# Transposed activations high, all weight buffers low in one pool, and products of zeros until the first weights

## The chip, the cores and the metric

The kernel runs on one core of a Trainium2 chip. The metric is device time in microseconds of one execution; a row of three such times is the measurement of the kernel before. Five engines work side by side, each on its own queue in the order in which the program lists its instructions: TensorE (PE: matrix products and transposes), VectorE (DVE), ScalarE (ACT), GpSimd (POOL) and SyncE (SP), which issues most DMA transfers. An instruction that has to wait holds up all behind it on its engine.

## What is computed

Two layers of a decoder on 256 tokens of width 1024, all in float32. Layer 0 mixes by sparse attention and differential attention, layer 1 by block-sparse attention; each is followed by an MLP of width 4096 with a squared ReLU.

```python
def rms_norm(x, g):
    xf = x.astype(jnp.float32)
    y = xf * lax.rsqrt(jnp.mean(xf * xf, axis=-1, keepdims=True) + EPS)
    return (y * g.astype(jnp.float32)).astype(x.dtype)

def sqrelu_mlp(hn, w1, w2):
    return jnp.square(jax.nn.relu(hn @ w1)) @ w2
...
    for i in range(DEPTH):
        hn = rms_norm(x, norm_mix[i])
        ...
            mix = odd_mixer(hn, od_w_in[o], od_w_out[o], bias_table)
        x = x + mix
        x = x + sqrelu_mlp(rms_norm(x, norm_mlp[i]), mlp_w1[i], mlp_w2[i])
    return rms_norm(x, norm_final)
```

## The kernel before

**Products.** Every float32 operand is split into a high part and a low rest in a reduced format (`hi`, `lo`), and a product is the sum of three: high by high, high by low, low by high (`mm3`, L552 to L554). An instruction row such as `ps<-whi,xTh` names the bank of the result and the two operands. The tokens lie in two tiles of 128 (t=0 and t=1).

**Weights.** The weights lie in one long array, in pieces of 128 rows by up to 1024 columns, in the order in which they are used. `loads` fetches a piece into one of five raw buffers; `splits` copies its high part on ScalarE (L492) and subtracts it on VectorE (L495). The parts go into six pairs of buffers. Three pairs (`whi`, `wlo`, the list `near`) lie low in the pool `hot`, at the start of each partition; three (`vhi`, `vlo`, the list `far`) lie high in the pool `consts`. In between lie the transposed x (`xTh`, `xTl`) and the attention's or MLP's transposed results (`mTh`, `mTl`). Each piece is marked as stationary or moving in its products, or as free; `region` lets a stationary piece take only a `far` pair, a moving one only a near pair (or a half of `mT` when that is lent out by `spare_m`), and a free one any. Pieces 4 and 5 of an output projection go into the two halves of `xT` (`ROOM`, `spare_x`).

**From x to its transpose.** `to_xT` scales x by the norm's weight on VectorE into a buffer P (L599), `turn_x` transposes four 128 by 128 blocks on TensorE (L615), copies the high part on ScalarE (L537) and the low part on VectorE (L543). The factor of the root mean square is made on its own (`rvar`, L585 to L587) and used later. The first norm is another: `first_norms` spreads the norm's weight over 128 partitions by two products with a row of ones (L919), takes the root mean square by a power on POOL (L579), and scales by both at once (L935).

**Order.** A planner (`Plan`) runs at build time. It holds an estimated duration for every step and starts on each engine the step of the lowest urgency number that is ready by its own clock; the instructions are written in that order. So a change of a buffer's rule changes the order of everything that the planner then sees ready earlier or later. `add_to_x` (L1335) adds an output projection's bank to x. `mlp` begins with two up-projections in which the tokens are stationary (`unit_N`), one for each token tile, and their results are transposed on TensorE (L1426).

**The start.** A tile of zeros is set, and six products of zeros of 512 columns (`WARM`) run on TensorE before the norm weight arrives.

Of the kernel before, what the change touches and what calls it, by code (L numbers as in the profile page):

```python
# [24 lines left out]
OP = mybir.AluOpType  # L25
# [48 lines left out]
def _blocks(ins):  # L74
# [44 lines left out]
    free = set(range(len(out)))  # L119

    def mlp(l):
# [7 lines left out]
        free.update(range(len(out), len(out) + TAIL))  # L129
# [3 lines left out]
    free.update(range(len(out), len(out) + 4))  # L133
# [5 lines left out]
    free |= set(range(len(out), len(out) + 4))  # L139
    out += [r(f["od_w_out"][0], i) for i in range(4)]  # L140
    mlp(1)
    cut, still = [], []
    for i, b in enumerate(out):
        stationary = None if i in free else b.ndim == 4
        b = np.ascontiguousarray(b).reshape(128, -1)
        k = 1 if b.shape[1] <= 1024 else 2
        cut += [np.ascontiguousarray(c) for c in np.split(b, k, 1)]
        still += [stationary] * k
    return cut, still


def _lay_out(ins):
    f = {k: np.asarray(ins[k]) for k in ins}
    blocks, still = _blocks(ins)
# [9 lines left out]
    for i, nm in enumerate(("ev_lam_q1", "ev_lam_q2", "ev_lam_k1", "ev_lam_k2")):  # L164
# [3 lines left out]
            "prm": prm, "gs": gs, "cst": _constants(), "eye": np.eye(128, dtype=np.float32)}, [(b.shape[1], s) for b, s in zip(blocks, still)]  # L168
# [3 lines left out]
NEAR = 3  # L172
RAWS, PARTS, NP, URGENT, TAIL, AHEAD = 5, 6, 5, 3, 3, 3
SECOND, ROOM, LATER = 5, (4, 5), (0, 0.05)
WARM, WRITE = 6, -1.5
# [147 lines left out]
class Slots:  # L323
# [5 lines left out]
    def get(self, n=1, only=None):  # L329
        ev = Event()  # L330
        self.waiting.append((ev, n, only))
# [25 lines left out]
    def serve(self):  # L357
        while self.waiting:
            ev, n, only = self.waiting[0]
            got = [i for i in self.items if only is None or only(i)][:n]  # L360
            if len(got) < n:
                return
            self.waiting.pop(0)
            self.items = [i for i in self.items if not any(i is g for g in got)]
# [10 lines left out]
def trunk_kernel(ctx: ExitStack, tc: tile.TileContext, x, w, prm_d, gs, cst_d, eye, out, widths):  # L375
    nc = tc.nc
    widths, still = zip(*widths)
# [13 lines left out]
    near = list(zip(tiles(NEAR, [128, 1024], F32R, "whi", hot), tiles(NEAR, [128, 1024], F32R, "wlo", hot)))  # L391
    tbuf = Slots(plan, list(zip(tiles(2, [128, 512], F32R, "Th", hot), tiles(2, [128, 512], F32R, "Tl", hot))))
    xT = (hot.tile([128, KT, S], F32R, name="xTh"), hot.tile([128, KT, S], F32R, name="xTl"))
# [5 lines left out]
    far = list(zip(tiles(PARTS - NEAR, [128, 1024], F32R, "vhi"), tiles(PARTS - NEAR, [128, 1024], F32R, "vlo")))  # L399
    parts = Slots(plan, [i for p in zip(near, far) for i in p] + near[len(far):] + far[len(near):])  # L400
# [42 lines left out]
    class Piece:  # L443
        count, current = 0, 0
# [5 lines left out]
        def use(self):  # L450
            Piece.current = max(Piece.current, self.p)

# [21 lines left out]
    def region(p):  # L474

        return None if still[p] is None else lambda it: any(it is f for f in far) == still[p]

# [1140 lines left out]
```

## Time and profile before

| | |
|---|---|
| three runs | 636.5, 638.49, 640.12 us, median 638.49 |
| the profiled execution | 636.71 us, of which 634.7 us is the span of the trace |
| busy in the span | PE 98%, PE weight load 89%, DVE 63%, ACT 56%, POOL 15% |
| granted TensorE clock, mean | 0.993 of full speed; in 40 slices of the span, 7 tenths in the first and 9 in all others |
| products of 256 columns with xT | 704 on each of three lines, some 283 ns each |
| DMA | 109.5 MB, mean 173 GB/s |

A busy time of a product is longer than its distance to the next product, because products overlap in the engine: the starts tell the pace. In a table of stretches, the clock column is the granted clock, 1.00 for 2.4 GHz and 0.50 for 1.2 GHz.

### The profile page before, as it was taken

The page shows a single profiled execution, that of the slowest core. Times are in us where ns is not written, and L with a number is a line of the kernel's source. Part 1 is how long each engine was busy: PE and PEld are TensorE (multiplying, and loading weights), DVE is VectorE, ACT ScalarE, POOL GpSimd, SP SyncE. Part 2 cuts the span into 40 slices and gives each one's busy share as a digit, 9 for nine tenths or more (in the row PEclk, how much of TensorE's full clock was granted, in tenths as well). Part 3 has the DMA queues.
Part 4 walks back from the last instruction along what each step waited for, and adds up shares of the span by engine and source line. Part 5 has one row for each costly group of instructions (what it writes and reads, how often), then busy time and mean ns, then how long its engine had stood idle before and what let it go on. Part 6 is the DMA issues. An engine that isn't in the chain of part 4 may idle for free.

```text
span 634.7 us, 10488 instructions
## 1 busy us (share of the span) xinstructions
PE 619.5 (98%) x4022; PEld 562.9 (89%) x4022; DVE 399.5 (63%) x722; ACT 354.3 (56%) x647; POOL 92.3 (15%) x111
## 2 busy tenths in 40 slices
PE   8989999899999999999999999999999999999995
PEld 6989899788889899998988999988889999898994
DVE  6899688958743535444576488895753545445264
ACT  5777478746744536343653488975654535345261
POOL 2022011120111211112110011210021211112011
PEclk7999999999999999999999999999999999999999
DMA  8864423514854564645646343562574564645421
GB/s 329 276 243 149 151 101 103 166 65 138 287 175 164 192 207 158 219 154 193 205 166 206 122 140 132 165 202 67 169 269 161 173 223 149 223 162 192 173 68 66
DMA packets 32100, 109.51 MB, mean 173 GB/s; under 512 B 3361, under 2 KB 5681, under 8 KB 32050
## 3 DMA queue, kind: packets, MB, share of 16 engines
q1 hardware_dynamic: 31186, 106.22, 49.8%
q0 software_dynamic: 576, 2.10, 1.1%
q8 instruction: 31, 0.51, 0.3%
q10 hardware_dynamic: 288, 0.52, 0.2%
q14 instruction: 19, 0.16, 0.1%
HBM read 107.76 MB, written 1.07 MB: 171 GB/s over the span
## 4 chain that ended last, share of the span: by engine, by line
PE 86%; DVE 7%; ACT 2%; issue 2%; DMA 2%; POOL 0%; POOLq 0%; DVEq 0%; ACTq 0%
PE ps L554 27%; PE ps L553 26%; PE ps L552 26%; PE ps L778 2%; DMA raw<-in_w_dram 2%; PE ps L812 1%; DVE wlo L495 1%; PE ps L615 1%; DVE vlo L495 1%; DVE mTl L980 1%; DVE Tl L543 1%; ACT P L792 0%; PE ps L519 0%; DVE x L1335 0%; DVE KZ L1014 0%
## 5 line engine op out<-in xcount | busy, mean ns | idle before, releaser
L495 DVE TENSOR_TENSOR vlo<-raw,vhi 128x1024 fp32r<-128x1024 f32 (+1 forms) x96 | 116.6, 1218 | 130.6 <-ACT vhi L492 130.3
L492 ACT ACTIVATE vhi<-raw 128x1024 fp32r<-128x1024 f32 (+1 forms) x96 | 100.3, 1049 | 157.1 <-PE ps L553 144.7
L552 PE MATMUL ps<-xTh,vhi 128*128 128x256 f32 x640 | 182.1, 285 | 0.0
L554 PE MATMUL ps<-xTh,vlo 128*128 128x256 f32 x640 | 181.1, 283 | 0.0
L553 PE MATMUL ps<-xTl,vhi 128*128 128x256 f32 x640 | 181.0, 283 | 0.0
L553 PEld LDWEIGHTS ps<-xTl,vhi 128*128 128x128 f32 x640 | 122.5, 191 | 1.2
L552 PEld LDWEIGHTS ps<-xTh,vhi 128*128 128x128 f32 x640 | 122.5, 191 | 1.2
L554 PEld LDWEIGHTS ps<-xTh,vlo 128*128 128x128 f32 x640 | 122.4, 191 | 0.0
L1398 POOL TENSOR_TENSOR P<-P 128x512 f32<-128x512 f32 x32 | 48.7, 1522 | 308.9 <-ACT P L1395 308.9
L495 DVE TENSOR_TENSOR wlo<-raw,whi 128x1024 fp32r<-128x1024 f32 (+1 forms) x65 | 77.6, 1209 | 9.6 <-ACT whi L492 9.5
L492 ACT ACTIVATE whi<-raw 128x1024 fp32r<-128x1024 f32 (+1 forms) x65 | 66.5, 1040 | 8.9 <-PE ps L554 7.2
L792 ACT ACTIVATE P<-P,nm 128x128 f32<-128x128 f32 x80 | 35.5, 447 | 8.6 <-DVE nm L788 8.5
L552 PE MATMUL ps<-whi,Th 128*128 128x512 f32 x100 | 39.0, 390 | 0.0
L553 PE MATMUL ps<-wlo,Th 128*128 128x512 f32 x100 | 39.0, 390 | 0.0
L554 PE MATMUL ps<-whi,Tl 128*128 128x512 f32 x100 | 38.9, 389 | 0.0
L495 DVE TENSOR_TENSOR mTl<-raw,mTh 128x1024 fp32r<-128x1024 f32 x30 | 35.9, 1219 | 0.1
L492 ACT ACTIVATE mTh<-raw 128x1024 fp32r<-128x1024 f32 x30 | 30.6, 1047 | 1.3 <-PE ps L554 1.3
L1400 DVE TENSOR_TENSOR Tl<-P,Th 128x512 fp32r<-128x512 f32 x22 | 15.2, 693 | 24.9 <-POOL P L1398 24.9
L1395 ACT ACTIVATE P<-ps 128x512 f32<-128x512 f32 x32 | 19.1, 597 | 15.9 <-PE ps L554 12.0
L788 DVE CUSTOM_DVE_ANT_0 P<-ps,B 128x128 f32<-128x128 f32 x80 | 24.5, 351 | 3.7 <-PE ps L778 3.5
L552 PE MATMUL ps<-mTh,Th 128*128 128x512 f32 x68 | 26.6, 391 | 0.0
L553 PE MATMUL ps<-mTl,Th 128*128 128x512 f32 x68 | 26.5, 390 | 0.0
(251 smaller groups left out, 1249.9 us busy)
## 6 DMA issues: line engine op xcount, KB each, us to landing
raw<-in_w_dram SPq DMA_DIRECT2D x192, 512.0 KB, 4.2
B<-ud SPq DMA_DIRECT2D x1, 2048.0 KB, 10.8
gB<-in_gs_dram POOLq DMA_DIRECT2D x4, 512.0 KB, 4.6
x<-in_x_dram SPq DMA_DIRECT2D x2, 512.0 KB, 4.6
raw<-in_w_dram SPq DMA_DIRECT2D x2, 420.0 KB, 5.5
out_dram<-P SPq DMA_DIRECT2D x2, 256.0 KB, 2.1
out_dram<-P ACTq DMA_DIRECT2D x2, 256.0 KB, 2.5
cst<-in_cst_dram SPq DMA_DIRECT2D x1, 372.0 KB
```

The costliest lines, as they stand in the source:

```text
L492: nc.scalar.activation(pc.hi[:, :n], raw[:, :n], AF.Copy)
L495: nc.vector.tensor_tensor(pc.lo[:, :n], raw[:, :n], pc.hi[:, :n].bitcast(F32), OP.subtract)
L543: nc.vector.tensor_tensor(lo, src, hi.bitcast(F32), OP.subtract)
L552: nc.tensor.matmul(out_, ah, bh, start=start, stop=False)
L553: nc.tensor.matmul(out_, ah, bl, start=False, stop=False)
L554: nc.tensor.matmul(out_, al, bh, start=False, stop=stop)
L778: nc.tensor.matmul(ps[:, 128 * qt:128 * qt + nk], q[:, par, ts], k[i][:, par, :nk], start=i == 0, stop=i == 1)
L788: nc.vector.tensor_tensor_reduce(P[:, c], ps[:, c], B[:, h, 0:nk][:, ::-1], -1.0, 3e38, OP.add, OP.min, nm[:, qt:qt + 1])
L792: nc.scalar.activation(P[:, c], P[:, c], AF.Exp, bias=nm[:, qt:qt + 1], scale=-1.0, accum_out=sums[:, qt:qt + 1])
L1395: e = act(t_act(512), lambda: nc.scalar.activation(r, b.t, AF.Relu), got, *deps)
L1398: g = pool(1.225, lambda: nc.gpsimd.tensor_tensor(sq, r, r, OP.mult), e)
L1400: h = dve(t_dve(512), lambda: nc.vector.tensor_tensor(hl, sq, hh.bitcast(F32), OP.subtract), f, g)
```

## The change

It has three parts.

1. *Places.* All six pairs of weight buffers are now `whi`, `wlo`, low in `hot`. The transposed x goes from `hot` to the pool `acts` high in the partition (`xTh` from byte 49,280 to 178,272). `near`, `far`, `region`, the marks of stationary pieces, and the choice of an item in `Slots.get` are gone: a piece takes the pair that has been free for longest.
2. *Zeros.* Two planned tasks (`keep_on`), with the highest urgency number, 9, emit products of zeros of 512 columns into bank 1 whenever the planner finds nothing else ready for TensorE, until four weight products have been emitted by a piece's count (`KEEP`).
3. *A planned duration.* The first norm's power on POOL is planned at 0.55 us and not 0.93. It costs the planner's clock only.

```diff
-NEAR = 3
...
-WARM, WRITE = 6, -1.5
+WARM, WRITE, KEEP = 6, -1.5, 4
...
-    near = list(zip(tiles(NEAR, [128, 1024], F32R, "whi", hot), tiles(NEAR, [128, 1024], F32R, "wlo", hot)))
+    parts = Slots(plan, list(zip(tiles(PARTS, [128, 1024], F32R, "whi", hot), tiles(PARTS, [128, 1024], F32R, "wlo", hot))))
...
-    xT = (hot.tile([128, KT, S], F32R, name="xTh"), hot.tile([128, KT, S], F32R, name="xTl"))
...
-    far = list(zip(tiles(PARTS - NEAR, [128, 1024], F32R, "vhi"), tiles(PARTS - NEAR, [128, 1024], F32R, "vlo")))
-    parts = Slots(plan, [i for p in zip(near, far) for i in p] + near[len(far):] + far[len(near):])
+    xT = (acts.tile([128, KT, S], F32R, name="xTh"), acts.tile([128, KT, S], F32R, name="xTl"))
...
         def use(self):
             Piece.current = max(Piece.current, self.p)
+            Piece.uses += 1
...
-    def region(p):
-
-        return None if still[p] is None else lambda it: any(it is f for f in far) == still[p]
-
...
-            got = pc.slots.get(only=region(p) if pc.slots is parts else None)
+            got = pc.slots.get()
...
+    def keep_on(z):
+
+        yield zero_e
+        while Piece.uses < KEEP:
+            yield pe(0.23, lambda: nc.tensor.matmul(banks[1].t, z[:, :128], z, start=True, stop=True), u=9)
+
+    for _ in range(2):
+        plan.spawn(keep_on(tbuf.items[1][0]))
...
-    def rstd(t, deps):
+    def rstd(t, deps, pow_t=0.93):
...
-            rs, e = rstd(t, [x_e[t]])
+            rs, e = rstd(t, [x_e[t]], 0.55)
```

The first place is the start of the program on TensorE. `Th1` is the tile of zeros, `P4` the row of ones with `gB` the norm's weight, L919 (L911 after) the spreading products, L615 (L607) the transposes, L552 to L554 (L544 to L546) the weight products, and `x6` counts equal rows. Before:

```order
L519 MATMUL ps7_117<-Th1_81 128x512 x6
L919 MATMUL ps2_112<-gB_125,P4_99 128x512
L919 MATMUL ps3_113<-gB_125,P4_99 128x512
L615 MATMUL ps4_114<-ident_121,P0_95 128x128 x4
L615 MATMUL ps5_115<-ident_121,P1_96 128x128 x4
L552 MATMUL ps0_110<-whi0_74,xTh_84 128x280
```

After:

```order
L502 MATMUL ps7_117<-Th1_87 128x512 x6
L508 MATMUL ps1_111<-Th1_87 128x512 x5
L911 MATMUL ps2_112<-gB_125,P4_103 128x512
L911 MATMUL ps3_113<-gB_125,P4_103 128x512
L508 MATMUL ps1_111<-Th1_87 128x512 x5
L607 MATMUL ps4_114<-ident_121,P0_99 128x128 x4
L508 MATMUL ps1_111<-Th1_87 128x512 x2
L607 MATMUL ps5_115<-ident_121,P1_100 128x128 x4
L508 MATMUL ps1_111<-Th1_87 128x512 x8
L544 MATMUL ps0_110<-whi0_74,xTh_104 128x280
```

Twenty zero products stand ahead of the first weight product (L508), and three more come behind it, 23 in all.

The second place is where layer 1's output projection ends and its MLP begins, on TensorE. Bank `ps1` takes the first up-projection of t=0, `ps0` that of t=1; `mTh`, `mTl` are the operands of the output projection. Before:

```order
L552 MATMUL ps4_114<-vhi0_100,mTh_86 128x512
L553 MATMUL ps4_114<-vlo0_103,mTh_86 128x512
L554 MATMUL ps4_114<-vhi0_100,mTl_87 128x512
L552 MATMUL ps1_111<-whi2_76,xTh_84 128x512
L553 MATMUL ps1_111<-wlo2_79,xTh_84 128x512
L554 MATMUL ps1_111<-whi2_76,xTl_85 128x512
...
L615 MATMUL ps7_117<-ident_121,P3_98 128x128 x4
```

After:

```order
L546 MATMUL ps1_111<-whi4_78,xTl_105 128x512
...
L544 MATMUL ps6_116<-whi0_74,mTh_90 128x512
L545 MATMUL ps6_116<-wlo0_80,mTh_90 128x512
L546 MATMUL ps6_116<-whi0_74,mTl_91 128x512
L1418 MATMUL ps4_114<-ident_121,P2_101 128x128 x2
L1418 MATMUL ps7_117<-ident_121,P2_101 128x128 x2
L607 MATMUL ps5_115<-ident_121,P0_99 128x128 x4
L607 MATMUL ps6_116<-ident_121,P4_103 128x128 x4
L544 MATMUL ps0_110<-whi1_75,xTh_104 128x512
L545 MATMUL ps0_110<-wlo1_81,xTh_104 128x512
L546 MATMUL ps0_110<-whi1_75,xTl_105 128x512
```

The 24 up-projection products of t=0, which came behind the last product of the output projection with the transposes among them, now come ahead of its last six products, and the transposes of t=1 come right behind those.

The third place is the same one on VectorE, after the change: the two additions to x of t=1 (L1327), the two scalings (L591), a weight split into `mTl` (L478), and the low part of the transposed x (L535).

```order
L1327 TENSOR_TENSOR x1_119<-ps5_115,x1_119 128x512
L1327 TENSOR_TENSOR x1_119<-ps6_116,x1_119 128x512
L591 TENSOR_TENSOR P0_99<-x1_119,gB_4248 128x512
L591 TENSOR_TENSOR P4_103<-x1_119,gB_4248 128x512
L478 TENSOR_TENSOR mTl_91<-raw1_95,mTh_90 128x1024
L535 TENSOR_TENSOR xTl_105<-ps5_115,xTh_104 128x4x128
...
L478 TENSOR_TENSOR mTl_91<-raw2_96,mTh_90 128x1024
L535 TENSOR_TENSOR xTl_105<-ps6_116,xTh_104 128x4x128
```

Before, the additions, scalings and the first weight split stood in the same order, with both low parts behind the second weight split.

## Rows read from the trace of the kernel before

**Rows 1.** The page: busy time, share and count by engine; chain that ended last.

```profile
PE 619.5 (98%) x4022; PEld 562.9 (89%) x4022; DVE 399.5 (63%) x722; ACT 354.3 (56%) x647; POOL 92.3 (15%) x111
...
PE 86%; DVE 7%; ACT 2%; issue 2%; DMA 2%; POOL 0%; POOLq 0%; DVEq 0%; ACTq 0%
```

**Rows 2.** PE groups by form: out<-in, shapes, count | busy us, mean ns | idle before.

```profile
L552 PE MATMUL ps<-xTh,vhi 128*128 128x256 f32 x640 | 182.1, 285 | 0.0
...
L552 PE MATMUL ps<-xTh,whi 128*128 128x256 f32 x64 | 18.9, 295 | 0.0
...
L552 PE MATMUL ps<-whi,xTh 128*128 128x512 f32 x40 | 16.2, 405 | 0.0
...
L552 PE MATMUL ps<-vhi,xTh 128*128 128x512 f32 x20 | 8.2, 409 | 0.0
```

**Rows 3.** Stretches: us; PE, PEld, DVE, ACT, POOL busy; PEclk, DMA, GB/s.

```profile
5.00:8.40 3.40, 3.21 (x14) 1.40 (x12) 2.50 (x4) 1.59 (x3) 0.72 (x2) 1.00 0.99 355
8.40:15.20 6.80, 6.09 (x27) 5.77 (x26) 6.56 (x10) 5.22 (x8) 0.75 (x2) 0.50 1.04 412
...
160.00:340.00 180.00, 180.00 (x1120) 162.75 (x1119) 96.18 (x100) 86.99 (x108) 29.33 (x23) 1.00 0.58 195
...
447.00:450.00 3.00, 3.00 (x17) 2.47 (x16) 3.00 (x5) 2.15 (x4) 0.00 (x0) 1.00 0.46 164
```

**Rows 4.** Timeline of PE at the start: start us, us, line, out<-in [idle before].

```profile
1.44 2.93 PE L519 MATMUL ps<-Th 128*128 128x512 f32 x6 [1.44 <-DVE Th L517]
4.30 2.31 PE L919 MATMUL ps<-gB,P 1*128 1x512 f32 x4
...
10.10 0.44 PE L552 MATMUL ps<-whi,xTh 128*128 128x280 f32 x1
10.33 0.44 PE L553 MATMUL ps<-wlo,xTh 128*128 128x280 f32 x1
...
15.54 0.30 PE L554 MATMUL ps<-whi,xTl 128*128 128x280 f32 x1
15.67 0.29 PE L552 MATMUL ps<-whi,xTh 128*128 128x280 f32 x1
...
16.32 0.30 PE L554 MATMUL ps<-whi,xTl 128*128 128x280 f32 x1
```

**Rows 5.** Timeline of DVE at the start.

```profile
5.87 1.52 DVE L935 SCALAR_TENSOR_TENSOR P<-x,rs,ps 128x512 f32<-128x512 f32 x2 [1.04 <-POOL rs L579]
...
10.35 1.03 DVE L495 TENSOR_TENSOR vlo<-raw,vhi 128x840 fp32r<-128x840 f32 x1
...
14.62 0.69 DVE L543 TENSOR_TENSOR xTl<-ps,xTh 128x512 fp32r<-128x512 f32 x1
```

**Rows 6.** Timeline of ACT at the start.

```profile
8.31 0.63 ACT L565 ACTIVATE scr<-x 128x512 f32<-128x512 f32 x1 [0.35 <-DMA x<-in_x_dram]
...
8.95 0.58 ACT L537 ACTIVATE xTh<-ps 128x512 fp32r<-128x512 f32 x1
9.42 0.89 ACT L492 ACTIVATE vhi<-raw 128x840 fp32r<-128x840 f32 x1
```

**Rows 7.** Timeline of PE where the second MLP begins.

```profile
446.64 0.39 PE L554 MATMUL ps<-vhi,mTl 128*128 128x512 f32 x1
446.87 0.39 PE L552 MATMUL ps<-whi,xTh 128*128 128x512 f32 x1
...
454.62 0.60 PE L1426 MATMUL ps<-ident,P 128*128 128x128 f32 x4
454.97 0.47 PE L552 MATMUL ps<-whi,xTh 128*128 128x512 f32 x1
...
455.51 0.39 PE L554 MATMUL ps<-whi,xTl 128*128 128x512 f32 x1
```

**Rows 8.** Timeline of DVE where the second MLP begins.

```profile
447.68 1.28 DVE L599 TENSOR_TENSOR P<-x,gB 128x512 f32<-128x512 f32 x2
...
450.01 0.14 DVE L586 TENSOR_SCALAR ms<-ssq 128x1 f32<-128x1 f32 x1
```

More of the change, by code (lines that the diff above doesn't have):

```diff
@@ L118, in _blocks @@
     out += [r(wo, i) for i in range(4)]
-    free = set(range(len(out)))
     def mlp(l):
@@ L128, in mlp @@
                 out.append(r(down, i - 1))
-        free.update(range(len(out), len(out) + TAIL))
         out.extend(r(down, i) for i in range(last, FF // 256))
     mlp(0)
-    free.update(range(len(out), len(out) + 4))
     for v in range(2):
@@ L138, in _blocks @@
         out.append(t(odd, span(128 * j, 128 * j + 128), span(1024 + 128 * j, 1152 + 128 * j)))
-    free |= set(range(len(out), len(out) + 4))
     out += [r(f["od_w_out"][0], i) for i in range(4)]
     mlp(1)
-    cut, still = [], []
-    for i, b in enumerate(out):
-        stationary = None if i in free else b.ndim == 4
+    cut = []
+    for b in out:
         b = np.ascontiguousarray(b).reshape(128, -1)
@@ L147, in _blocks @@
         cut += [np.ascontiguousarray(c) for c in np.split(b, k, 1)]
-        still += [stationary] * k
-    return cut, still
+    return cut
 def _lay_out(ins):
     f = {k: np.asarray(ins[k]) for k in ins}
-    blocks, still = _blocks(ins)
+    blocks = _blocks(ins)
     prm = np.zeros((128, P_N), np.float32)
@@ L167, in _lay_out @@
     return {"x": np.ascontiguousarray(f["x"].reshape(S, D)), "w": np.concatenate([b.reshape(-1) for b in blocks]),
-            "prm": prm, "gs": gs, "cst": _constants(), "eye": np.eye(128, dtype=np.float32)}, [(b.shape[1], s) for b, s in zip(blocks, still)]
-NEAR = 3
+            "prm": prm, "gs": gs, "cst": _constants(), "eye": np.eye(128, dtype=np.float32)}, [b.shape[1] for b in blocks]
 RAWS, PARTS, NP, URGENT, TAIL, AHEAD = 5, 6, 5, 3, 3, 3
 SECOND, ROOM, LATER = 5, (4, 5), (0, 0.05)
-WARM, WRITE = 6, -1.5
+WARM, WRITE, KEEP = 6, -1.5, 4
 ORDER = ["vg", "k", "q0", "c", "q1", "h", "dv", "d0", "d1", "d2", "d3"]
@@ L327, in __init__, with get @@
         self.plan, self.items, self.waiting, self.wanted = plan, list(items), [], []
-    def get(self, n=1, only=None):
+    def get(self, n=1):
         ev = Event()
-        self.waiting.append((ev, n, only))
+        self.waiting.append((ev, n))
         self.serve()
@@ L357, in serve @@
     def serve(self):
[L358 to L364, printed above, removed]
+        while self.waiting and len(self.items) >= self.waiting[0][1]:
+            ev, n = self.waiting.pop(0)
+            got, self.items = self.items[:n], self.items[n:]
             self.plan.fire(ev, "slot", got if n > 1 else got[0])
@@ L376, in trunk_kernel @@
     nc = tc.nc
-    widths, still = zip(*widths)
     hot = ctx.enter_context(tc.tile_pool(name="hot", bufs=1))
@@ L443, in trunk_kernel @@
     class Piece:
-        count, current = 0, 0
+        count, current, uses = 0, 0, 0
         def __init__(self):
@@ L578, in rstd @@
             ms = both
-        return rs, pool(0.93, lambda: nc.gpsimd.tensor_tensor(rs, ms, half[:, 0:1], OP.pow), e, half_e, u=-4)
+        return rs, pool(pow_t, lambda: nc.gpsimd.tensor_tensor(rs, ms, half[:, 0:1], OP.pow), e, half_e, u=-4)
     def rvar(t, deps):
```

## The prediction

> **What bounds the kernel now.** I read the page's busy shares first, then its chain of work that ended last. TensorE is busy 619.5 of the 634.7 us of the span, and products make up nearly all of the chain [rows 1]. The table of stretches shows where that holds: 160 to 340 us is full to the last digit, and so are the three microseconds on which the second MLP begins [rows 3]. In such places only two things move the end: a product that takes longer or shorter from start to start, or a product that has to wait. The start is different. Before 15.2 us TensorE has idle time, and the granted clock falls to 0.50 from 8.4 to 15.2, that is to 1.2 of 2.4 GHz, after a stretch in which TensorE was busy 3.21 of 3.40 us [rows 3]. So I ask three things: does the place of an operand change the pace of a product, what do the zero products do to the start, and what does the new order do where no slack is left.
>
> **Part 1, the places.** The kernel before is its own experiment, since it has weights in both places. With the transposed x low, 640 products of 256 columns take weights from high buffers (named v) and 64 from low ones (named w): mean 285 and 295 ns. With 512 columns it is 409 high against 405 low [rows 2]. Which operand moves and which stays is swapped between these two pairs. The differences are 4 and 10 ns, of opposite sign, in means that hold waiting too. I take 0 for the move of the transposed x, of the weights, and of the smaller buffers that go along. The bound on both sides comes from the starts. At 512 columns they are 0.23 us apart (446.64 to 446.87 [rows 7]), and 512 columns at 2.4 GHz are 0.213, so 14 ns of each product are not columns. The 256-column products are 640 + 64 on each of the three lines of a product, 2112 in all. If a place could take these 14 ns away, or double them, that would be 30 us either way. No row here shows a part of it, so it stays a rival, not a term.
>
> Any piece may now go into any buffer. Before, a moving piece waited for a low one and a stationary piece for a high one. Where TensorE is full for 180 us [rows 3] a split that comes sooner is worth nothing. Zero.
>
> **Part 2, the zeros at the start.** There are 23 new products of 512 columns on TensorE, in its order: 5 before the two products that spread the norm's weight, 5 before the first transposes, 2 between these, 8 before the first weight product, 2 and 1 further on. Orders on VectorE and ScalarE are as before there. The price of one is 0.23 us at the full clock [rows 7] and 0.48 at half (the six old ones run from 1.44 to 4.30 [rows 4]).
>
> Walk it. From 4.30: two zeros at 0.48, three at 0.23, 1.65 us, so the spreading products start at 5.95. They took 2.31 before [rows 4]; with 0.7 of that at half clock I take 2.0, so the first bank is there at 6.95 and the second at 7.95. VectorE's scaling (0.76 each, 5.87 before [rows 5]) runs 6.95 to 7.7 and 7.95 to 8.7. TensorE: 5 zeros to 9.1, four transposes (0.35, from 454.62 to 454.97 [rows 7]) to 9.45, two zeros, four transposes to 10.25, 8 zeros to 12.1. ScalarE copies the first half of the transposed x to 10.05 (0.58), squares the second half of x to 10.7 (0.63), copies the second half to 11.25 (0.58) [rows 6], then a weight piece to 12.15 (0.89 [rows 6]). VectorE's split of that piece stood at 10.35 and now stands at 12.15, +1.8. From there VectorE works without a gap up to the split of the second token tile at 14.62 [rows 5], which goes to 16.4 and ends (0.69) at 17.1.
>
> What TensorE does meanwhile: 24 weight products, 8 transposes and 3 zeros after 12.1. At full clock (0.13 from start to start, 15.54 to 15.67 [rows 4]) these are 3.1 + 0.7 + 0.7 = 4.5, so the second token tile's first product could start at 16.6 and its third at 16.85. The third needs the split that ends at 17.1. Before, it started at 16.32 [rows 4]. Shift: **+0.8**, and 0.2 for hand-overs between engines that the durations leave out (my estimate): +1.0. From there on TensorE is full [rows 3], and nothing gives it back.
>
> The gain is in it already: 18 or so of the weight products ran 0.23 apart (10.10 to 10.33 [rows 4]) and now run 0.13 apart, 1.8 us. It pays for the zeros on TensorE almost wholly, and the chain over ScalarE and VectorE then sets the time. The bounds: if the first five zeros all run at full speed and the hand-overs are free, TensorE's own work ends at 16.35 and the shift is 0.0. If the clock falls at 8.4 again and rises at 15.2 as before [rows 3], the 6.8 us do 3.4 us of the above; TensorE then stands at 11.8 of the walk at 15.2 and the third product comes at 20.3, +4.0.
>
> The Trainium skill (TensorE: Matmul & The Clock Gate, section Why this matters for your kernels) says that TensorE has to be kept busy without gaps to get the higher level, and that idle gaps lose it. By that rule the zeros hold the clock and the shift is the +1.0. The trace agrees only in part: the level was lost after the 3.21 busy of 3.40 us [rows 3], so by the row alone it may be lost once more, and the shift would be +4.0.
>
> **Part 3, the order at the second MLP.** With six equal buffers the planner has up-projection weights ready earlier, and puts all 24 products of the first token tile's first up-projection ahead of the last six products of the attention's output projection. Before, they came after these. They were the cover for a chain: the last output projection adds to x, x is scaled, transposed, split, and only then can the second token tile start. In the trace that chain is hidden, TensorE is busy 3.00 of 3.00 us [rows 3]. Now there is nothing behind the last projection but 4 + 8 transposes and two products.
>
> The chain, from the end of the last projection's column time (446.87 [rows 7]): the second addition ends and scaling begins at 447.68; scaling and one split of a weight piece, which VectorE has queued next in both orders, are over at 450.01 [rows 8]; then one split of the transposed x, 0.69 [rows 5], is 450.70. That is 3.83. TensorE has 3 x 0.35 of transposes and 0.54 of two products (454.97 to 455.51 [rows 7]), 1.59. It waits 3.83 - 1.59 = **2.2 us** for the low part. The second half of the split comes some 2 later, behind another weight piece, and TensorE has ten products (2.3) till then. Bounds: the split of a weight piece takes some 1.1 of the 2.33 us in [rows 8], after 1.28 of scaling. Without it in the way the wait is 1.1; with the second weight piece ahead too, it is 3.3. In the first MLP the order of TensorE is the old one, and the same chain is covered.
>
> **Sum.** +1.0 + 2.2 + 0 = +3.2 us. The profiled run took 636.71, of which 634.7 is span; it becomes 639.9. The median of the runs shown is 638.49, 1.8 above that run, and the same +3.2 gives 641.7. A measurement of this kernel tells about 0.5% (3.2 us) from no change, so the forecast sits on that edge.
>
> **Rivals.** *The zeros are free and the chain is shorter* (not slower). The start's shift is 0.0, its lower bound, and the weight split at the second MLP lies ahead of the addition in time, so the wait is 1.1: 639.6; with only one of the two, 640.6. For it: the shift at the start is two near-equal paths, 16.85 and 17.1. Against it: VectorE works in its written order, and the weight split stands behind the scaling. It decides if VectorE's split of the second token tile starts before 15.7. Chance 0.30.
>
> *The clock falls again.* The zeros then cost twice their price and the start moves by 4.0: 638.49 + 4.0 + 2.2 = 644.7. For it: the fall at 8.4 behind a busy stretch [rows 3]. Against: that stretch was a mix of short products and transposes with gaps, the new one is zeros end to end. This is also the case in which the change doesn't do what it says. Chance 0.13.
>
> *The place does matter.* Low weights with a high x is the pair that the trace has only mirrored. A tenth of the 30 us is enough for a verdict: 635.5 with the wait and shift as above and 6 us gained, or 648 with 6 lost. Only the equality of the pairs speaks against it [rows 2]. Chance 0.12, half to each side.
>
> **How the numbers follow.** The forecast has 0.45: 641.7, between 640.5 and 643.5, 0.25 of it beyond the 0.5%. Faster: 0.06 of the places and 0.02 of the free zeros, 0.08. Slower: 0.25, 0.13 and 0.06, with 0.01 for runs that scatter as those shown, 0.45. Within 0.5%: 0.47. The range takes the forecast, the free zeros and the clock: 637.0 (a gain of what a run scatters below the free zeros) to 645.0.
>
> **What would show it.** Right in part 1: products of 512 columns start 0.23 us apart as before, and the MLP stretches keep their length. In part 2: a granted clock of 1.00 through 8.4 to 15.2, first weight product at 12, third product of the second token tile near 17.3. In part 3: one wait of TensorE of about 2 us for the split of the transposed x as the second MLP begins, and none at the first MLP. Wrong: a stretch of 0.50 after 8.4, a wait under 1 us at the second MLP, or MLP stretches that are longer or shorter at no idle time.

## The result and the profile after

The changed kernel takes 645.12 us (median of 14 runs, 643.68 to 650.96). The kernel before took 639.85 us in the same comparison (14 runs, 636.32 to 643.9). The ratio is 1.0099, with a 95% interval of 1.0071 to 1.0127: the change costs 4.5 to 8.1 us, 6.3 in the middle. The ratio goes by the means of the runs; the medians lie 5.3 apart. The forecast said 641.7, 3.2 us more than before; its sign was right and its size about half. The measured time lies 0.1 us above the range.

The profiled execution of the changed kernel took 645.73 us, its span 643.6, 8.9 more than the span of before. The page's busy time of TensorE and its row of the granted clock, in 40 slices of the span:

```profile
PE 626.4 (97%) x4045; PEld 565.6 (88%) x4045; DVE 407.0 (63%) x723; ACT 360.4 (56%) x647; POOL 79.3 (12%) x110
...
PEclk8999999989999999999999999999999999999998
```

TensorE has 23 products more and 6.9 us more busy time than in [rows 1]. Apart from its last slice, where the work ends, the clock row dips twice: in the first slice, as before, and once more in the ninth. The table of stretches gives both (columns as in [rows 3]):

```profile
5.00:8.70 3.70, 3.70 (x12) 1.89 (x11) 1.48 (x3) 0.90 (x1) 0.55 (x1) 1.00 0.98 366
8.70:12.10 3.40, 3.40 (x14) 2.81 (x13) 2.27 (x5) 1.21 (x3) 0.19 (x1) 0.50 1.03 417
12.10:18.90 6.80, 6.80 (x47) 6.30 (x47) 5.89 (x8) 5.34 (x10) 0.56 (x1) 1.00 0.70 231
...
128.20:135.00 6.80, 6.80 (x26) 6.02 (x26) 5.64 (x18) 3.96 (x13) 1.39 (x3) 0.50 0.50 166
```

From 5.0 to 18.9 TensorE has no idle time at all, and still it runs at 1.2 GHz from 8.7 to 12.1. The start on its timeline, to be read beside [rows 4]:

```profile
5.95 1.98 PE L911 MATMUL ps<-gB,P 1*128 1x512 f32 x4
7.86 1.80 PE L508 MATMUL ps<-Th 128*128 128x512 f32 x5
9.46 1.06 PE L607 MATMUL ps<-ident,P 128*128 128x128 f32 x4
...
11.88 2.21 PE L508 MATMUL ps<-Th 128*128 128x512 f32 x8
13.93 0.29 PE L544 MATMUL ps<-whi,xTh 128*128 128x280 f32 x1
...
18.89 0.29 PE L546 MATMUL ps<-whi,xTl 128*128 128x280 f32 x1
```

The last of these is the product that stood at 16.32 before. TensorE's waits, by what they waited for (us in total, times, longest):

```profile
PE ps L544 <- DVE KZ L1006: 2.9, 1, 2.9
PE ps L545 <- DVE Tl L535: 2.6, 2, 2.1
...
PE ps L607 <- DVE P L591: 0.9, 1, 0.9
PE ps L804 <- DVE P L841: 0.7, 1, 0.7
...
PE ps L545 <- DVE xTl L478: 0.3, 1, 0.3
...
PE ps L546 <- DVE ms L578: 0.3, 1, 0.3
```

The first and the longer of the second's two were there before, at 2.7 and 2.0; the others are new. These two lie in the first attention: the one that the profile puts down to VectorE's `KZ` at 124 us (119 before), the one for a low part `Tl` at 49 us (45 before). L607 is the transpose of t=1 where the second MLP begins, and the wait of L546 comes just behind it. L804 is a transpose in the first attention. The wait for `xTl` is at 428.9 us, in layer 1's output projection, for a piece of weights that lies in a half of the transposed x.

To see where the 8.9 us come from, I follow five places that both kernels have, by the start of a product (us), and the end. Unit k is the projection to the keys, the first whose products have 256 columns. The last two columns are two experiments told below: each kernel with its two long waits filled.

| place | before | after | more | before, filled | after, filled | more |
|---|---|---|---|---|---|---|
| first product of unit k (the start is over) | 19.84 | 22.45 | 2.61 | 20.06 | 22.17 | 2.11 |
| product behind the wait for KZ | 122.50 | 126.81 | 4.31 | 123.93 | 126.54 | 2.61 |
| first transposes of the first MLP's norm | 146.79 | 153.46 | 6.67 | 148.18 | 150.81 | 2.63 |
| first transposes of layer 1's norm | 326.07 | 332.26 | 6.19 | 327.51 | 329.62 | 2.11 |
| first transposes of the second MLP's norm | 443.25 | 449.16 | 5.91 | 444.65 | 446.51 | 1.86 |
| last product | 627.33 | 636.26 | 8.93 | 628.73 | 633.60 | 4.87 |

So 2.6 us are lost at the start, 1.7 in the first attention, 2.4 behind the wait for KZ (where the clock is low from 128.2 to 135.0), 0.5 are won back in the first MLP, and 2.7 are lost from layer 1's norm on, 3.0 of them behind the second MLP's norm against 0.3 won ahead of it (what this 0.3 hides is told below, under layer 1's attention).

### The profile page after: what moved, and what is told of

Read it like the earlier page. It is cut to its first block, busy times and chain, and to the rows that moved or that the text cites. A ratio compares the mean times of both kernels' runs of the same rounds, so it can differ in the third digit from the quotient of the medians.

```text
span 643.6 us, 10584 instructions
## 1 busy us (share of the span) xinstructions
PE 626.4 (97%) x4045; PEld 565.6 (88%) x4045; DVE 407.0 (63%) x723; ACT 360.4 (56%) x647; POOL 79.3 (12%) x110
## 4 chain that ended last, share of the span: by engine, by line
PE 85%; DVE 8%; ACT 2%; DMA 2%; issue 2%; POOL 1%; POOLq 0%; ACTq 0%; DVEq 0%
PE ps L545 26%; PE ps L546 26%; PE ps L544 26%; DVE wlo L478 2%; PE ps L770 2%; DMA raw<-in_w_dram 2%; PE ps L804 1%; PE ps L607 1%; PE ps L508 1%; DVE Tl L535 1%; ACT P L784 1%; ACT whi L475 1%; DVE P L780 1%; DVE xTl L478 1%; POOL P L841 1%
## 5 line engine op out<-in xcount | busy, mean ns | idle before, releaser
L478 DVE TENSOR_TENSOR wlo<-raw,whi 128x1024 fp32r<-128x1024 f32 (+1 forms) x157 | 190.0, 1220 | 71.4 <-ACT whi L475 70.9
L475 ACT ACTIVATE whi<-raw 128x1024 fp32r<-128x1024 f32 (+1 forms) x157 | 162.8, 1051 | 95.9 <-PE ps L546 65.2
L544 PE MATMUL ps<-xTh,whi 128*128 128x256 f32 x592 | 168.7, 285 | 0.0
L546 PE MATMUL ps<-xTh,wlo 128*128 128x256 f32 x592 | 166.3, 281 | 0.0
L545 PE MATMUL ps<-xTl,whi 128*128 128x256 f32 x592 | 166.2, 281 | 0.0
L545 PEld LDWEIGHTS ps<-xTl,whi 128*128 128x128 f32 x592 | 111.7, 189 | 0.7
L544 PEld LDWEIGHTS ps<-xTh,whi 128*128 128x128 f32 x592 | 111.5, 188 | 0.7
L546 PEld LDWEIGHTS ps<-xTh,wlo 128*128 128x128 f32 x592 | 111.5, 188 | 0.0
L478 DVE TENSOR_TENSOR mTl<-raw,mTh 128x1024 fp32r<-128x1024 f32 x34 | 41.6, 1224 | 22.9 <-ACT mTh L475 22.9
L1392 DVE TENSOR_TENSOR Tl<-P,Th 128x512 fp32r<-128x512 f32 x22 | 15.2, 692 | 50.3 <-POOL P L1390 50.3
L546 PE MATMUL ps<-whi,Tl 128*128 128x512 f32 x120 | 46.9, 390 | 0.0
L544 PE MATMUL ps<-whi,Th 128*128 128x512 f32 x120 | 46.7, 390 | 0.0
L544 PE MATMUL ps<-xTh,mTh 128*128 128x256 f32 (+1 forms) x128 | 38.5, 301 | 0.0
L545 PE MATMUL ps<-xTl,mTh 128*128 128x256 f32 (+1 forms) x128 | 38.1, 297 | 0.3 <-DVE xTl L478 0.3
L546 PE MATMUL ps<-xTh,mTl 128*128 128x256 f32 (+1 forms) x128 | 38.0, 297 | 0.0
L544 PE MATMUL ps<-whi,xTh 128*128 128x512 f32 (+1 forms) x88 | 34.2, 389 | 0.1
L546 PE MATMUL ps<-whi,xTl 128*128 128x512 f32 (+1 forms) x88 | 33.3, 378 | 0.3 <-DVE ms L578 0.3
```

The lines of the kernel that those rows point to most:

```text
L475: nc.scalar.activation(pc.hi[:, :n], raw[:, :n], AF.Copy)
L478: nc.vector.tensor_tensor(pc.lo[:, :n], raw[:, :n], pc.hi[:, :n].bitcast(F32), OP.subtract)
L544: nc.tensor.matmul(out_, ah, bh, start=start, stop=False)
L545: nc.tensor.matmul(out_, ah, bl, start=False, stop=False)
L546: nc.tensor.matmul(out_, al, bh, start=False, stop=stop)
L1392: h = dve(t_dve(512), lambda: nc.vector.tensor_tensor(hl, sq, hh.bitcast(F32), OP.subtract), f, g)
```

## Experiments

All times are medians against the kernel before as it ran in the same comparison (639.98, 640.34, 640.06 and 640.0 us). The ratio goes by means, so it can differ from that of the medians.

| kernel | us | ratio (95%) | differs from before by |
|---|---|---|---|
| z_alone | 644.0 | 1.0074 (1.0047 to 1.0101) | zeros and planned power |
| p_alone | 643.1 | 1.0058 (1.0032 to 1.0084) | all but the zeros |
| c_places | 639.89 | 0.9995 (0.9974 to 1.0017) | places alone |
| o_alone | 641.19 | 1.0030 (1.0006 to 1.0054) | rule of buffers alone |
| q_alone | 640.3 | 1.0011 (0.9983 to 1.0040) | planned power alone |
| z_nopow | 642.86 | 1.0040 (1.0014 to 1.0067) | zeros alone (25) |
| z_early | 640.65 | 0.9997 (0.9974 to 1.0020) | 6 zeros |
| z_late | 642.68 | 1.0037 (1.0010 to 1.0063) | 20 zeros |
| a_half | 643.07 | 1.0075 (1.0044 to 1.0105) | the change, zeros half as long |
| a_cover | 646.73 | 1.0105 (1.0067 to 1.0142) | the change, other order at the second MLP |
| fill_b | 637.63 | 0.9970 (0.9947 to 0.9993) | two waits filled |
| fill_c | 635.91 | 0.9941 (0.9921 to 0.9961) | places, two waits filled |
| fill_q | 638.37 | 0.9990 (0.9967 to 1.0013) | planned power, filled |
| fill_o | 640.06 | 1.0000 (0.9978 to 1.0021) | rule, filled |
| fill_z | 639.77 | 1.0002 (0.9979 to 1.0025) | zeros, filled |
| fill_a | 643.74 | 1.0054 (1.0032 to 1.0075) | the change, filled |

### The change taken apart

z_alone adds the zeros and the planned power to the kernel before:

```diff
+        while Piece.uses < KEEP:
+            yield pe(0.23, lambda: nc.tensor.matmul(banks[1].t, z[:, :128], z, start=True, stop=True), u=9)
...
-            rs, e = rstd(t, [x_e[t]])
+            rs, e = rstd(t, [x_e[t]], 0.55)
```

> The kernel before with the zeros and the shorter planned power, places and rule of buffers as before. Theory A (read from the two traces: the zeros cost 2.6 us at the start, since the clock falls behind them too, and a little more in the first attention, where the plan is moved): +2.5 to +3.5 us, and 3.4 more in runs in which the clock also falls at 128 us. Theory B (the recorded walk): +1.0 us. Theory C (the clock that falls at 128 us comes from the places or the order, not from the zeros): +2.6 us and no fall at 128 us in the trace.

It came out 4.0 us above. Its unit k starts at 22.71, and its clock is at 0.50 from 9.4 for 3.4 us and from 128.8 for 6.8. So theory C fell: the fall at 128 us comes without the new places and the new order.

p_alone is the changed kernel with `KEEP` at 0:

```diff
-WARM, WRITE, KEEP = 6, -1.5, 4
+WARM, WRITE, KEEP = 6, -1.5, 0
```

> The changed kernel without the zeros (KEEP 0): places and free choice of buffers as changed. Theory A (the order at the second MLP costs 2.2, each MLP gains 0.7 from the places): +0.8 us. Theory B (order 2.2, places nothing): +2.2 us. Theory C (the fall of the clock at 128 us belongs to places or order): +4 us or more, with that fall in the trace.

3.1 us above, more than A and B said, and with the clock low in two stretches behind the two long waits, as its table of stretches shows (columns as in [rows 3]):

```profile
48.10:54.90 6.80, 6.70 (x32) 6.70 (x32) 4.86 (x19) 2.17 (x8) 1.67 (x3) 0.50 0.22 75
126.60:136.80 10.20, 9.68 (x34) 8.40 (x35) 7.75 (x24) 6.34 (x22) 1.39 (x3) 0.50 0.56 190
```

With no zeros at all the clock falls at 128 us too, and in q_alone below, which has nothing but the planned power, from 127.3 for 3.4 us. It belongs to no part of the change alone.

c_places has the new places with the old rule; every engine's order is that of before.

```diff
-    xT = (hot.tile([128, KT, S], F32R, name="xTh"), hot.tile([128, KT, S], F32R, name="xTl"))
...
-    far = list(zip(tiles(PARTS - NEAR, [128, 1024], F32R, "vhi"), tiles(PARTS - NEAR, [128, 1024], F32R, "vlo")))
+    far = list(zip(tiles(PARTS - NEAR, [128, 1024], F32R, "vhi", hot), tiles(PARTS - NEAR, [128, 1024], F32R, "vlo", hot)))
+    xT = (acts.tile([128, KT, S], F32R, name="xTh"), acts.tile([128, KT, S], F32R, name="xTl"))
```

> The kernel before with only the places changed (all weight buffers low in one pool, the transposed x high); the rule of which piece takes which pair stays, and the order of all engines is the same as before, row by row. Theory A: -1.5 us, from some 700 products in each MLP that start about 1 ns earlier each. Theory B: 0. A rival on the other side: the places cost in the attention stages, +1 us or more.

No difference in time, 0.9995. The interval takes in A and B. The trace tells them apart (below, with fill_c).

o_alone drops the rule and keeps the places:

```diff
-            got = pc.slots.get(only=region(p) if pc.slots is parts else None)
+            got = pc.slots.get()
```

> The kernel before with only the rule removed: any piece takes any pair, places as before, no zeros. Only the order changes, from the first MLP on. Theory A and B: +2.2 us, all of it as one wait where the second MLP begins. Theory C (the order also moves something in the attention of layer 1): another number there, and a difference before 440 us.

1.2 us above, with an interval from 0.4 to 3.5. Its trace has the same new waits as the changed kernel: 0.9 for P and 0.3 behind it at the second MLP, and 0.3 for the weights in `xTl` in layer 1's output projection. So theory C holds beside A and B: the order also moves something in layer 1's attention.

### What the planned power and the zeros cost

q_alone changes only the planned duration.

```diff
-            rs, e = rstd(t, [x_e[t]])
+            rs, e = rstd(t, [x_e[t]], True)
...
-        return rs, pool(0.93, lambda: nc.gpsimd.tensor_tensor(rs, ms, half[:, 0:1], OP.pow), e, half_e, u=-4)
+        return rs, pool(0.55 if first else 0.93, lambda: nc.gpsimd.tensor_tensor(rs, ms, half[:, 0:1], OP.pow), e, half_e, u=-4)
```

> The kernel before with only the planned duration of the first norm's power cut from 0.93 to 0.55 us; no zeros, places and rule as before. 67 rows of TensorE's order change, all in the first attention. Theory A (in the traces of the runs so far, everything with this number is some 1.8 us later between 40 and 60 us, at full clock): +1.8 us, in the first attention alone. Theory B (the recorded one: it moves the planner's clock only and costs nothing): 0.

The time doesn't tell: 1.0011, from -1.1 to +2.6 us. fill_q below does better.

z_nopow has the zeros without the planned power (`rstd(t, [x_e[t]])` as before).

> The kernel before with the zeros (25 of them, by the unchanged planned power) and nothing else. Theory A (the zeros cost the start 2.5 to 3 us and nothing further on): +2.5 us, and the first attention as before. Theory B (the recorded walk of the start): +1.0 us. Theory D (the reorder of the first attention comes from the zeros, not from the planned power): +4 us.

2.5 us above, as A had it. The first product of unit k starts at 23.13.

z_early stops the zeros when the spreading products are emitted, z_late starts them there.

```diff
-        while Piece.uses < KEEP:
+        while not spread:
```

> The kernel before with zeros only until the spreading products: five ahead of them and one behind. Theory A (each zero ahead of the spreading products delays the chain over VectorE and ScalarE, and the clock still falls behind them): +1.5 us, half of the cost of all zeros. Rival E (the zeros behind the spreading products cost it all, since they stand in front of the transposes): 0.

```diff
+        yield spread
         while Piece.uses < KEEP:
```

> The kernel before with zeros only behind the spreading products: seven, one, eight and three. Theory A: +1.5 us, the other half. Rival E: +2.5 us, all of the cost. Theory F (zeros keep the clock up here, and pay for themselves): 0 or below.

z_early is where before is, z_late 2.3 above, as rival E had it; each interval reaches some 1.5 us to either side, so z_early is just below the half that theory A gave it, and z_late fits both. Unit k starts at 20.70 in z_early and at 22.75 in z_late, against 19.84 before. So most of the cost comes of the zeros in front of the transposes and the weight products. The start of z_late on TensorE's timeline:

```profile
8.01 3.22 PE L529 MATMUL ps<-Th 128*128 128x512 f32 x7
11.07 0.60 PE L628 MATMUL ps<-ident,P 128*128 128x128 f32 x4
```

The seven zeros start 0.43 apart behind the first, so the engine is at half its pace (3.22 us for seven, 2.21 for eight at 11.88 in the changed kernel), and the transposes come at 11.07. In c_places, which runs its start at that pace too and has no zeros there, they come at 8.01.

a_half is the changed kernel with zeros of 256 columns:

```diff
-            yield pe(0.23, lambda: nc.tensor.matmul(banks[1].t, z[:, :128], z, start=True, stop=True), u=9)
+            yield pe(0.23, lambda: nc.tensor.matmul(banks[1].t[:, :256], z[:, :128], z[:, :256], start=True, stop=True), u=9)
```

> The changed kernel with zeros of 256 columns in place of 512, the same 23 of them in the same order. Theory A (TensorE's own queue sets the start, so zeros cost what they take): 23 x 0.107 us at the full clock and more at half, the start 2.5 us shorter than that of the changed kernel, as early as without zeros. Theory B (the chain over VectorE and ScalarE sets the start): less than 1 us shorter. Rival G (shorter zeros let the clock fall for longer, and that costs as much): no gain.

Its zeros in front of the weight products, the first of these, and the first product of unit k, on TensorE's timeline:

```profile
9.27 2.06 PE L508 MATMUL ps<-Th 128*128 128x256 f32 x8
11.12 0.43 PE L544 MATMUL ps<-whi,xTh 128*128 128x280 f32 x1
...
19.72 0.28 PE L544 MATMUL ps<-xTh,whi 128*128 128x256 f32 x1
```

Unit k starts at 19.72 and not at 22.45: 2.7 us back for zeros of half the length, as theory A had it. It is also no later than the 19.84 of before, so zeros of half the length pay for themselves. The time doesn't tell: its ratio gives 2.8 to 6.7 us above before, that of the changed kernel 4.5 to 8.1, so I use the trace here.

### The order at the second MLP

a_cover is the changed kernel with one number of the planner changed.

```diff
-SECOND, ROOM, LATER = 5, (4, 5), (0, 0.05)
+SECOND, ROOM, LATER = 5, (4, 5), (0, 0)
```

> The changed kernel with one number of the planner changed (LATER from (0, 0.05) to (0, 0)): the output projection of the second token tile in layer 1 is no longer put behind the up-projection, so that up-projection products again stand behind its last product and can cover the chain over VectorE. Theory A (the wait where the second MLP begins is the missing cover): 2.6 us less than the changed kernel, +3 to +3.5 us against the kernel before, and no wait at that place. Rival (the wait moves to the first up-projection of the first token tile): as the changed kernel, +6 us.

In the trace the waits for P and for the low parts are gone from the list, and from the first transposes of the second MLP's norm (449.31) to the last product (635.01) it takes 185.70 us against 187.10: 1.4 less, not 2.6. The time shows none of it: 646.73, from six runs of which four lie at 646.45 or above. So the cover's place is confirmed in the trace, and the size of the gain stays open. Shorter waits are left: t=1's transposes come at 456.72, 0.52 behind the start of the product before them, where products start 0.23 apart.

### The two waits

fill_b puts products of zeros into the two waits in the first attention, at 45 and 119 us. They go into a sum that is open at that point, and add nothing to it.

```diff
+    def fill(out_, b, n):
+        for _ in range(n):
+            nc.tensor.matmul(out_[:64], VH[:, 0, 0, 64:128], b, start=False, stop=False)
...
+            fill(bank.t, pc.hi[:, 512 * n:512 * n + 512], FILL.get(len(calls), 0))
...
-            mm3(o, (v[0][:, kt, c], v[1][:, kt, c]), (T[0][:, m], T[1][:, m]), start and kt == 0, stop and kt == 1)
+            mm3(o, (v[0][:, kt, c], v[1][:, kt, c]), (T[0][:, m], T[1][:, m]), start and kt == 0, stop and kt == 1,
+                17 if len(maps) == 1 and kt == 0 else 0)
```

> The kernel before with 17 products of zeros of 256 columns in the wait at 45 us and 12 of 512 columns in the wait at 119 us, each into an open sum, to which they add nothing; the order of all else is unchanged. Theory H (these two waits are what makes the clock fall behind them, at 48 and at 125 to 128 us, in some runs): no stretch at 1.2 GHz but at the start and after the end, the times of the runs closer together, and the median 1 to 1.5 us below the kernel before. Rival I (the falls have another cause, or the fills are too late in the queue and cost their own time): no change or slower, with falls at the same places.

TensorE's timeline at the two waits:

```profile
46.19 2.10 PE L552 MATMUL ps<-Th,G 128*64 128x256 f32 x17
48.60 0.39 PE L558 MATMUL ps<-Tl,G 128*128 128x256 f32 x1 [0.31 <-DVE Tl L543]
...
121.04 2.92 PE L552 MATMUL ps<-whi,G 128*64 128x512 f32 x12
123.93 0.50 PE L556 MATMUL ps<-vhi,mTh 128*128 128x512 f32 x1
```

And the stretch around the second wait in the table of stretches, where the changed kernel was at 0.50:

```profile
118.00:140.00 22.00, 22.00 (x118) 17.00 (x118) 17.14 (x51) 14.83 (x46) 5.33 (x11) 1.00 0.43 144
```

Theory H holds. The products behind the waits start no earlier for it, but the clock stays at 1.00, the runs lie between 636.14 and 639.18 (before: 636.44 to 642.36 beside them), and the median is 2.4 us lower, with an interval of 0.4 to 3.4, which takes in the 1 to 1.5 of the theory. Of the twelve profiled executions without fills, ten show the clock fall to 0.50 at the end of one of these two waits or of both (from 0.5 us ahead of the end to 1.8 behind it); of the six with fills, none does. That is also what the 128.20 to 135.00 row of the changed kernel is.

fill_c is the same on c_places.

> The same two fills on the kernel before with only the places changed. Theory A and H together (places -1.3, fills -1 to -1.5): 2.3 to 2.8 us below the kernel before, faster than both kernels. Theory B and I: no difference.

4.15 us below before, and 1.7 below fill_b. It is the fastest kernel of this study. Both have the same order on every engine, so the first MLP can be measured end to end. In fill_b from its first product of 256 columns to the next norm's first transposes:

```profile
163.19 0.28 PE L556 MATMUL ps<-xTh,vhi 128*128 128x256 f32 x1
...
327.51 0.71 PE L620 MATMUL ps<-ident,P 128*128 128x128 f32 x5
```

In fill_c:

```profile
162.40 0.28 PE L556 MATMUL ps<-xTh,vhi 128*128 128x256 f32 x1
...
325.91 1.04 PE L620 MATMUL ps<-ident,P 128*128 128x128 f32 x8
```

164.32 against 163.51, 0.81 less, with TensorE full in both. In the second MLP, to the last product, it is 168.17 against 167.37. The kernel before and c_places give the same four lengths (164.31, 163.51, 168.17, 167.37). So the places do matter, by 0.8 us in each MLP. The other kernels agree: the first MLP takes 164.31 or 164.32 us in all eleven traces with the old places, and 163.51 to 163.73 in all seven with the new ones. In fill_b the products of 256 columns start 119.84 ns apart on average between 170 and 320 us, in fill_c 118.29; those of 512 columns start 227.8 and 228.5 apart, so the whole gain comes of the former.

### Each part on the quiet base

fill_q, fill_o, fill_z and fill_a put the same two fills on q_alone, o_alone, z_nopow and the changed kernel; the edits are those above, taken together.

> The two fills (which took the scatter of the clock away) on the kernel before with the planned power of 0.55 us alone. The kernel with the fills alone stood 2.4 us below the kernel before. Theory A (the reorder of the first attention costs 1.3 us): -1.1 us against the kernel before. Theory B (nothing): -2.4 us.

> The two fills on the kernel before with the rule of buffers removed. Theory A (the order at the second MLP costs 2.5 us): +0.1 us against the kernel before. Rival (the order's cost is the clock's scatter): -2.4 us.

> The two fills on the kernel before with the 25 zeros at the start. Theory A (the zeros cost the start some 2.7 us): +0.3 us against the kernel before. Theory B (the recorded 1.0): -1.4 us.

> The two fills on the changed kernel. Theory A (zeros 2.6, planned power 1.3, order 2.5, places -1.3 to -1.8, they add up): 4.6 to 5.1 us above the kernel before with fills, which is +2.2 to +2.7 us against the kernel before, and no fall of the clock at 48 or 128 us. Rival: what the changed kernel lost beyond 3.2 us was the fall of the clock at 128 us alone: then with fills 3.2 above, +0.8 us.

Against fill_b, each by its distance to before (fill_b stands at -2.4): the planned power +0.8 (-1.6), the rule +2.5 (+0.1), the zeros +2.2 (-0.2), the places -1.7, the whole change +6.2 (+3.7). Each of the ratios is uncertain by some 1.4 us, that of fill_b too. The zeros and the rule came out as A said. The planned power is between A and B, and neither is ruled out. The whole is above both of its theories; A's +2.2 to +2.7 lies within its interval (+2.0 to +4.8), the rival's +0.8 does not. The four parts make 3.8, and the whole is 6.2; by the times the two may agree.

The traces tell more. At the last product the filled change is 4.87 us behind fill_b, and the four parts alone make 2.3 there. Most of that gap arises ahead of the first MLP's norm, where single executions scatter: from unit k to that norm fill_b takes 128.1 us, fill_o and fill_z 127.4 and 127.3, fill_c 126.5, with the same order on TensorE. Behind that norm the parts make 1.6 (the rule 2.8, the places -1.2, the others 0.0) and the whole 2.2. So some 0.7 come only of the parts together.

## Why the prediction was right and wrong

**Part 1, the places: wrong, at zero.** It took the pairs of [rows 2] as equal, and they are, to some ns, but they are busy times, and all have one of the two operands in the place of before. The step that failed is the last one: that pairs in the trace which swap place and role cover a pair that the trace doesn't have. It was named as a rival with up to 30 us; it measures 0.8 us per MLP, 1.6 together, shown by two pairs of kernels with equal order: 1.6 ns of the 119.8 from start to start at 256 columns, and not up to 14.

**Part 2, the zeros: the sign right, the term mis-sized.** The walk gave +1.0; the trace has +2.6, the quiet base 2.1 (and 2.2 in time). Kernels without the new zeros start unit k anywhere between 19.80 and 20.77, so these are good to some 0.5. Up to the spreading products the walk gave 5.95 and 5.95 was measured, with some luck: the zeros began at 4.17 and not at 4.30, and a zero at half the clock takes 0.43 and not 0.48 (the 0.48 is a mean with the first one's 0.59 in it), but three of the five were slow and not two. The step that failed is that the zeros run at the full clock. Behind the spreading products the clock fell to 1.2 GHz, from 8.7 to 12.1, half as long as the 6.8 us of [rows 3]. The first weight product came at 13.93 and not 12.1, which is 1.8 late; the rest of the walk, from there to the third product of the second token tile, took 4.96 us, foreseen 5.0. The walk had VectorE's chain as the later of two near-equal paths. With half the clock TensorE's own queue was the later one: it is busy 6.80 of 6.80 us up to 18.9, and a_half, with shorter zeros, gives all of it back in its trace. The rival in which the clock falls again was right in kind, and half in length.

The Trainium skill (TensorE: Matmul & The Clock Gate, section Why this matters for your kernels), by which work without gaps keeps the higher level, was weighed there as the reason to expect the clock to hold. At the start the trace speaks against it: 3.70 of 3.70 us busy, 1.98 of them with the spreading products that use one row of the array, and then 0.50. At the two long waits the trace agrees in kind, though not in each execution: without fills ten of twelve lose the level at one of these gaps or both, with fills none of six.

A second look at the gain that part 2 counted. The first weight product and unit k of the kernel before:

```profile
8.02 0.40 PE L552 MATMUL ps<-whi,xTh 128*128 128x280 f32 x1
...
19.84 0.28 PE L552 MATMUL ps<-xTh,vhi 128*128 128x256 f32 x1
```

From one to the other it takes 11.82 us, with the clock at 0.50 up to 15.2. In a_half, with the clock at 1.00 from 11.67 on, it takes 8.60, in the changed kernel 8.52. So the gain is there, 3.2 to 3.3 us, more than the 1.8 of the walk: the later start also spares TensorE a wait of 0.7 us that it had at 9.70. But the zeros and the slow stretch among them put the first weight product 5.9 us later (13.93) in the changed kernel, and only 3.1 later (11.12) in a_half.

**The planned power: left out of the sum without a check of the order.** The change was described as moving the planner's clock only, and the sum had no term for it. It reorders 67 rows of TensorE in the first attention, with new waits of 0.7 us for P and 0.5 for a low part `Tl` (q_alone and fill_q have both): the planner now lets VectorE do a scaling that GpSimd did. What it costs isn't shown: it is 0.8 us on the quiet base by time, with some 1.4 to either side, and 0.6 at the last product; the whole change loses 0.5 in the first attention there, less than executions with one order differ (0.8).

**Part 3, the order: right in place and size.** TensorE at the second MLP, beside [rows 7]:

```profile
459.55 0.39 PE L546 MATMUL ps<-whi,mTl 128*128 128x512 f32 x1
459.78 0.60 PE L1418 MATMUL ps<-ident,P 128*128 128x128 f32 x4
461.32 1.26 PE L607 MATMUL ps<-ident,P 128*128 128x128 f32 x8 [0.94 <-DVE P L591]
462.67 0.50 PE L544 MATMUL ps<-whi,xTh 128*128 128x512 f32 x1
463.00 0.40 PE L545 MATMUL ps<-wlo,xTh 128*128 128x512 f32 x1
463.66 0.50 PE L546 MATMUL ps<-whi,xTl 128*128 128x512 f32 x1 [0.26 <-DVE ms L578]
```

And VectorE, beside [rows 8]:

```profile
459.30 1.38 DVE L1327 TENSOR_TENSOR x<-ps,x 128x512 f32<-128x512 f32 x2 [3.12 <-PE ps L546]
460.59 1.28 DVE L591 TENSOR_TENSOR P<-x,gB 128x512 f32<-128x512 f32 x2
461.79 1.22 DVE L478 TENSOR_TENSOR mTl<-raw,mTh 128x1024 fp32r<-128x1024 f32 x1
462.92 0.68 DVE L535 TENSOR_TENSOR xTl<-ps,xTh 128x512 fp32r<-128x512 f32 x1
```

From the end of the last projection (459.78, where the transposes behind it start) to the third product (463.66) are 3.88 us; the walk had 3.83. Less TensorE's own 1.59 that is 2.3 us of waiting, foreseen 2.2. The rule alone shows the same: from the second MLP's norm to the last product fill_o takes 187.61 us and fill_b 184.08; less six products that fill_o has more there (1.4 us) that is 2.1. It is spread over three places (for P, between the two fours of transposes, for the low part), not one wait as the prediction said it would look. Against it stands the 0.8 of the places in the MLP behind it, so the whole stage shows less.

**Not foreseen at all: the clock at 128 us.** In the profiled run of the changed kernel it makes 2.4 us between the second and third place of the table (4.31 to 6.67); with fills the differences at these two places are 2.61 and 2.63. It is not part of the change, since the kernels before and after both have the wait. It is also much of why runs of either scatter by 7 us: with the fills the changed kernel's lie within 2.8, and those of before within 3.0. The profiled execution of before, 636.71, had no such fall and lay near the lowest of its runs, while its 14 runs have a median of 639.85.

**Layer 1's attention.** At the second MLP's norm the filled change is 1.86 behind, but its output projection then has six more products to do (1.4 us) than in the old order, so it really stands 3.2 behind, 1.1 more than at layer 1's norm. The free choice of buffers costs most of this inside the attention: by the same count o_alone and fill_o, with the rule gone and nothing else, lose 0.7 there, 0.3 of it the wait for the weights in `xTl`; c_places loses nothing. The remaining 0.4 comes only with places and rule together, and its cause stays open. The prediction looked only at the attention's end.

**The sum.** Foreseen 1.0 + 2.2 + 0. On the quiet base, by the traces: 2.1 at the start, 0.5 in the first attention, -0.5 in the first MLP, 1.1 in layer 1's attention, 2.3 at the second MLP and -0.8 in it, 4.7 of the 4.87 measured. The steps that failed are thus the zeros at full clock (1.1 too little), the places at zero (-0.5 and -0.8), and the order's cost inside layer 1's attention (1.1), which had no term; the 0.5 of the first attention is within the scatter there. The measured time is farther from 641.7 for another reason too: the forecast started from the median of three runs, 638.49, and fourteen give 639.85.

## What to carry to other kernels

Filler on an engine with an in-order queue is paid at the clock that rules there, by all that stands behind it (zeros of 512 columns cost the start 2.1 to 2.6 us, zeros of 256 nothing); put it where the engine waits, behind nothing that could run, as the two fills are (2.4 us gained, and half of the scatter), and not in front of the first useful work. A change of a rule or of a planned duration in a planner moves work far from where it stands, so compare the orders of all stages and not only of those that the change names. When runs of a kernel scatter more than a part is worth, take away the cause of the scatter first and measure the parts on the quiet base.

## What was not expected of the hardware

In ten of twelve executions without fills a wait of TensorE of 2.1 to 2.9 us goes with 3.4 to 10.2 us at 1.2 GHz. The fall comes between 0.5 us ahead of the wait's end and 1.8 behind it, so mostly with TensorE busy again: 6.80 of 6.80 us at 0.50 in the changed kernel. Of the 24 waits of these two kinds in the twelve executions, 13 have it. At the start the clock fell behind 3.70 us of uninterrupted work. The record of the granted clock doesn't show everything there: it says 1.00 for c_places from 8.0 to 14.8, while the weight products of that kernel start 0.23 us apart up to 14.04 and 0.13 apart from 15.67 on, so in the first microseconds the pace has to be read from the starts:

```profile
13.81 0.43 PE L553 MATMUL ps<-vlo,xTh 128*128 128x280 f32 x1
14.04 0.41 PE L554 MATMUL ps<-vhi,xTl 128*128 128x280 f32 x1
...
15.67 0.29 PE L553 MATMUL ps<-wlo,xTh 128*128 128x280 f32 x1
15.80 0.29 PE L554 MATMUL ps<-whi,xTl 128*128 128x280 f32 x1
```

And the same products in the same order take 0.5% less time with low weights and a high transposed x (163.51 against 164.32 us in an MLP); which of the moved buffers does it wasn't tried.
